# Seven block products instead of eight in three of the eleven units of each down-projection

## The chip, the cores and the metric

The kernel runs on one core of a Trainium2 chip. The metric is the device time of one execution in microseconds (us); lower is better. A core has a matrix engine (TensorE, "PE" in the profile; "PEld" is its load of the stationary operand), VectorE (DVE), ScalarE (ACT), GpSimd (POOL), and SyncE (SP), whose queue issues nearly all transfers from device memory here. TensorE writes its results to PSUM, which is split into eight banks of 128 x 512 f32 values.

## What is computed

Two layers of a decoder over 256 tokens with 1024 features. Each layer has an attention and a feed-forward part with a causal convolution of width 3; a final norm ends it. The change is in the last product of the feed-forward part, `@ w_down`, with 2816 rows of weights and 1024 columns:

```python
def conv_ffn(h, w_up, conv_w, conv_b, w_down):
    S_ = h.shape[1]
    u = h @ w_up
    up = jnp.pad(u, ((0, 0), (CONV_W - 1, 0), (0, 0)))
    u = conv_b + sum(conv_w[j] * up[:, j:j + S_] for j in range(CONV_W))
    gate, val = jnp.split(u, 2, axis=-1)
    return (jax.nn.silu(gate) * val) @ w_down
...
        x = x + conv_ffn(rmsnorm(x, ffn_norm[l]), w_up[l], conv_w[l], conv_b[l], w_down[l])
```

## The kernel before

**Numbers in two parts.** Every f32 operand of a product is split into a high part, rounded to the type that TensorE multiplies, and a low part, the rest. A product of two operands takes three matmuls: high by high, high by low, low by high.

**Weights.** All weights come as units of 128 x 2048 f32 (1 MB) from one packed array, in the order of use. `fetch(i)` (L165 to L170) issues the transfer of a unit into one of 3 raw buffers `wr`. `prepare(i)` (L197 to L217) makes the parts: ScalarE copies raw to high (`hi_part`, L181), VectorE takes raw minus high (`lo_part`, L189, or L191 where a gain is multiplied in, as in the units of the K/V projection), in 2 or 4 pieces; the last step fetches unit i+3. There are 4 buffers for the high and 4 for the low parts, `wh` and `wl`. `used(i)` says that TensorE has taken its last matmul of unit i and starts `prepare(i + 4)`. So a unit's parts can be written as soon as the unit four places before it is consumed.

**Order.** The program is written against a planned clock that counts ideal TensorE time (`tick`). Side work is put on a list as a `chain` of steps with due times; a step's instructions are emitted when the planned clock passes them, or at once where `need` or `require` asks for them. Each engine then runs its own instructions strictly in the order of emission, as early as their inputs and buffers allow. Steps of `prepare` start no closer than 4500 ns to each other by this clock (L203).

**The feed-forward part** (`ffn`, L661 to L761). 22 up units make gate and value features, 48 matmuls of 256 columns each. `post` (L700 to L732) follows each: three taps of the convolution (ACT L715, DVE L719 and L721), the Silu on ACT (L725), the product with the value on POOL (L726), and the split into parts, hi on ACT (L730) and lo on DVE (L731). Two consecutive results share a tile of 128 x 1024, a "quad", of which the pool has 15. Then `Down` (L569) runs the 11 down units. A down unit has 2 blocks of 128 rows (k), each with 1024 columns, that is two column halves n of 512; the activations have two blocks b of 128 tokens. That makes 2 x 2 x 2 = 8 block products, 24 matmuls with 512 columns (L587, L588, L590), added up over all units in four PSUM banks `acc[b][n]`. `units` runs units 0 to 8; `finish` runs units 9 and 10 bank by bank, and as each bank is complete `add` (L652) adds it to the residual `xr` on VectorE and starts what follows (`after`: squares for the norm on ACT, transposes on TensorE (L288) and their split into parts, on ACT L297 and DVE L298). In layer 0 the K/V projection follows (L345 to L347); in layer 1 the final norm, with POOL multiplying by the final gain (L1057). Four further PSUM banks, tags `u` and `t` with two each, serve the up units and the transposes; between unit 0 and the first `after` of a down-projection nobody uses them.

Of the kernel before, what the change touches and what calls it, by code (L numbers as in the profile page):

```python
# [51 lines left out]
U_DN0 = U_UP0 + NF  # L52
U_KV = U_DN0 + NF // 2
U_QB = U_KV + 2
U_OB = U_QB + 4
U_UP1 = U_OB + 4
U_DN1 = U_UP1 + NF
N_UNITS = U_DN1 + NF // 2


@with_exitstack
def trunk(ctx: ExitStack, tc, x, xw, pos, cpk, fin, w, out):
# [116 lines left out]
    def hi_part(i, c):  # L179
        g = gain_of(i, c)  # L180
        nc.scalar.activation(wq[i][0][:, c], raws[i][:, c], AF.Copy, **({} if g is None else {"scale": g}))  # L181
# [41 lines left out]
    def need(i):  # L223
        require("w", i)
# [344 lines left out]
    class Down:  # L569


        def __init__(self, u, n_u, parts, wait, short=False):
            self.u, self.n_u, self.parts, self.wait, self.short = u, n_u, parts, wait, short
            self.acc = None

        def mm(self, i, k, b, cols, last=1):
            if self.acc is None:
                self.acc = [[bank("acc") for _ in range(2)] for _ in range(NB)]
            need(self.u + i)
            self.wait(i)  # L580
            hi, lo = wq[self.u + i]
            ph, pl = self.parts[2 * i + k]
# [8 lines left out]
            tick(len(cols) * 3 * 512 / 2.4)  # L591

        def units(self, lo, hi):
            for i in range(lo, hi):
                for k in range(2):
                    for b in range(NB):
                        self.mm(i, k, b, range(2))
                        yield 6 * 512 / 2.4
                used(self.u + i)

        def finish(self, i0, after, tail=None, by_half=False):
# [26 lines left out]
            for i in range(i0, self.n_u):  # L628
                used(self.u + i)

        def end(self, b, n, tail):
# [4 lines left out]
            nc.vector.tensor_tensor(out=x_, in0=self.acc[b][n], in1=x_, op=ALU.add)  # L636
            need(self.u + i)
            self.wait(i)
            wh, wl = wq[self.u + i]
            for m in range(2):  # L640
# [20 lines left out]
    def ffn(layer, u_up, u_dn, hT, y, rb, after, tail=None):  # L661
# [37 lines left out]

        def post(i, up, pq):  # L700
            hi, lo = pq[:, 2 * (i % 2)], pq[:, 2 * (i % 2) + 1]
            t = [row3(S) for _ in range(2)]
            gs, h = row3(S), row3(S)
            w0, w1, w2, bb = ([cp[:, CW + (layer * 2 * NF + j * NF + i) * 4 + k:][:, :1] for j in range(2)] for k in range(4))
# [19 lines left out]
            def gate():  # L724
                nc.scalar.activation(gs, t[0], AF.Silu)  # L725
                nc.gpsimd.tensor_tensor(out=h, in0=gs, in1=t[1], op=ALU.mult)  # L726

            steps = [(200.0, scale), (700.0, tap2)] if i < n_raw else [(200.0, tap2)]
            chain(("p", i), *steps, (400.0, taps), (1600.0, gate),
                  (3400.0, lambda: nc.scalar.activation(hi, h, AF.Copy)),  # L730
                  (450.0, lambda: nc.vector.tensor_tensor(out=lo, in0=h, in1=f(hi), op=ALU.subtract)))  # L731
            parts.append((hi, lo))  # L732

        pq = quad()
# [9 lines left out]
        for i in range(2, NF):  # L744
            if i % 2 == 0:
                pq = quad()
# [5 lines left out]
        def wait(i):  # L752
            require("p", 2 * i)
            require("p", 2 * i + 1)

        if tail is not None:
            nc.sync.dma_start(fin_t, fin.partition_broadcast(P))
        dn = Down(u_dn, NF // 2, parts, wait, tail is not None)
        for _ in dn.units(0, NF // 2 - 2):
# [346 lines left out]
def pack(inp):  # L1106
# [19 lines left out]

    def rows2(mat):
        mm = k_major(mat)
        for i in range(mm.shape[0] // 2):
            units.append(turns(mm[2 * i:2 * i + 2]).transpose(1, 0, 2).reshape(P, UNIT))  # L1130

# [8 lines left out]
    up(inp["w_up"][0])  # L1140
    rows2(inp["w_down"][0])
    halves(turns(k_major(inp["w_kv_b"])))
# [6 lines left out]
    up(inp["w_up"][1])  # L1149
    rows2(inp["w_down"][1])  # L1150
    assert len(units) == N_UNITS
    wpk = np.stack(units)
# [39 lines left out]
```

## Time and profile before

| what | value |
|---|---|
| median of 3 runs (lowest, highest) | 547.92 us (547.56, 548.28) |
| span of the profiled execution | 545.6 us |
| granted TensorE clock, mean | 0.998 |
| down-projection of layer 0 in the profile | 230.6 to about 288 us |
| matmuls, and loads of the stationary operand | 3742 and 3742 |
| bytes read from device memory | 99.30 MB |

The profile is of one execution. Its span runs from the first to the last instruction; no time of its own is given for that execution beyond the span, so the 2.3 us between span and median are what lies around it. Busy time of TensorE counts overlapping, pipelined matmuls, so the distance between the starts of matmuls says more than their durations (379 ns for 512 columns). A group's "idle before" is time in which the engine stood still before instructions of the group, and the name behind it is who ended the wait.

### The profile page before, as it was taken

The page shows a single profiled execution, that of the slowest core. Times are in us where ns is not written, and L with a number is a line of the kernel's source. Part 1 is how long each engine was busy: PE and PEld are TensorE (multiplying, and loading weights), DVE is VectorE, ACT ScalarE, POOL GpSimd, SP SyncE. Part 2 cuts the span into 40 slices and gives each one's busy share as a digit, 9 for nine tenths or more (in the row PEclk, how much of TensorE's full clock was granted, in tenths as well). Part 3 has the DMA queues.
Part 4 walks back from the last instruction along what each step waited for, and adds up shares of the span by engine and source line. Part 5 has one row for each costly group of instructions (what it writes and reads, how often), then busy time and mean ns, then how long its engine had stood idle before and what let it go on. Part 6 is the DMA issues. An engine that isn't in the chain of part 4 may idle for free.

```text
span 545.6 us, 9917 instructions
## 1 busy us (share of the span) xinstructions
PE 537.5 (99%) x3742; PEld 493.9 (91%) x3742; DVE 416.9 (76%) x868; ACT 372.6 (68%) x731; POOL 131.6 (24%) x166
## 2 busy tenths in 40 slices
PE   8999999999999999999999999999999999999995
PEld 7888888899999999988888887789999999998884
DVE  6798778689798888864467788799899888884414
ACT  6989776678577777744357798797567777663314
POOL 8322102013322233220001165202332332210003
PEclk9999999999999999999999999999999999999999
DMA  8974445342556565666553534242375656666201
GB/s 317 401 268 175 167 154 181 129 155 79 199 211 217 223 220 195 208 227 231 178 208 135 179 150 156 77 155 91 142 264 201 214 193 217 249 229 220 109 0 77
DMA packets 16464, 100.99 MB, mean 185 GB/s; under 512 B 1952, under 2 KB 2080, under 8 KB 5920
## 3 DMA queue, kind: packets, MB, share of 16 engines
q1 hardware_dynamic: 16128, 100.09, 50.8%
q8 instruction: 29, 0.48, 0.3%
q10 hardware_dynamic: 288, 0.26, 0.1%
q14 instruction: 19, 0.16, 0.1%
HBM read 99.30 MB, written 1.05 MB: 184 GB/s over the span
## 4 chain that ended last, share of the span: by engine, by line
PE 90%; ACT 5%; DVE 3%; issue 1%; DMA 1%; DVEq 0%; POOL 0%; ACTq 0%
PE acc L590 8%; PE acc L587 8%; PE acc L588 8%; PE u L681 7%; PE u L682 7%; PE u L680 6%; PE t L681 6%; PE t L682 6%; PE t L680 6%; PE acc L345 5%; PE acc L346 5%; PE acc L347 5%; ACT m L468 2%; PE acc L792 2%; PE acc L682 2%; PE acc L681 2%
## 5 line engine op out<-in xcount | busy, mean ns | idle before, releaser
L189 DVE TENSOR_TENSOR wl<-wr,wh 128x1024 fp32r<-128x1024 f32 (+1 forms) x186 | 202.4, 1108 | 49.0 <-ACT wh L181 48.7
L181 ACT ACTIVATE wh<-wr 128x1024 fp32r<-128x1024 f32 (+1 forms) x190 | 176.5, 957 | 50.3 <-PE acc L590 42.2
L726 POOL TENSOR_TENSOR m<-m,m 128x256 f32<-128x256 f32 x44 | 69.1, 1571 | 167.8 <-DVE m L721 89.4
L587 PE MATMUL acc<-wh,q 128*128 128x512 f32 x238 | 92.2, 387 | 0.2 <-ACT q L545 0.2
L588 PE MATMUL acc<-wl,q 128*128 128x512 f32 x238 | 90.6, 381 | 0.0
L680 PE MATMUL u<-q,wh 128*128 128x256 f32 x320 | 88.3, 277 | 0.0
L681 PE MATMUL u<-q,wh 128*128 128x256 f32 x320 | 88.2, 276 | 0.1
L682 PE MATMUL u<-q,wl 128*128 128x256 f32 x320 | 87.9, 275 | 0.0
L680 PE MATMUL t<-q,wh 128*128 128x256 f32 x288 | 79.2, 275 | 0.0
L681 PE MATMUL t<-q,wh 128*128 128x256 f32 x288 | 79.2, 275 | 0.0
L682 PE MATMUL t<-q,wl 128*128 128x256 f32 x288 | 79.2, 275 | 0.0
L590 PE MATMUL acc<-wh,q 128*128 128x512 f32 x238 | 74.9, 380 | 0.0
L681 PEld LDWEIGHTS u<-q,wh 128*128 128x128 f32 x320 | 61.4, 192 | 0.3 <-DVE q L309 0.3
L682 PEld LDWEIGHTS u<-q,wl 128*128 128x128 f32 x320 | 61.4, 192 | 0.0
L680 PEld LDWEIGHTS u<-q,wh 128*128 128x128 f32 x320 | 61.3, 192 | 0.0
L680 PEld LDWEIGHTS t<-q,wh 128*128 128x128 f32 x288 | 55.3, 192 | 0.0
L681 PEld LDWEIGHTS t<-q,wh 128*128 128x128 f32 x288 | 55.3, 192 | 0.0
L682 PEld LDWEIGHTS t<-q,wl 128*128 128x128 f32 x288 | 55.3, 192 | 0.0
L587 PEld LDWEIGHTS acc<-wh,q 128*128 128x128 f32 x238 | 45.0, 189 | 7.0 <-ACT q L545 0.6
L590 PEld LDWEIGHTS acc<-wh,q 128*128 128x128 f32 x238 | 44.8, 190 | 6.2 <-issue 0.2
L588 PEld LDWEIGHTS acc<-wl,q 128*128 128x128 f32 x238 | 45.1, 189 | 5.8 <-issue 0.2
L345 PE MATMUL acc<-wh,q 128*128 128x512 f32 x128 | 50.0, 391 | 0.0
(182 smaller groups left out, 1008.7 us busy)
## 6 DMA issues: line engine op xcount, KB each, us to landing
wr<-in_w SPq DMA_DIRECT2D x82, 1024.0 KB, 4.8
wr<-in_w SPq DMA_DIRECT2D x16, 512.0 KB, 6.2
first<-in_xw SPq DMA_DIRECT2D x7, 384.0 KB, 6.0
xr<-in_x SPq DMA_DIRECT2D x2, 512.0 KB, 7.9
fin_t<-in_fin SPq DMA_DIRECT2D x1, 512.0 KB, 5.7
out<-ot SPq DMA_DIRECT2D x1, 512.0 KB, 2.6
first<-in_xw SPq DMA_DIRECT2D x1, 388.0 KB, 3.5
out<-m ACTq DMA_DIRECT2D x1, 256.0 KB, 2.1
```

The costliest lines, as they stand in the source:

```text
L181: nc.scalar.activation(wq[i][0][:, c], raws[i][:, c], AF.Copy, **({} if g is None else {"scale": g}))
L189: nc.vector.tensor_tensor(out=lo, in0=raw, in1=hi, op=ALU.subtract)
L345: nc.tensor.matmul(o, xh[:, blk(b)], wh, start=(c == 0), stop=False)
L346: nc.tensor.matmul(o, xh[:, blk(b)], wl, start=False, stop=False)
L347: nc.tensor.matmul(o, xl[:, blk(b)], wh, start=False, stop=(c == KC - 1))
L587: nc.tensor.matmul(o, ph[:, blk(b)], turns(hi[:, s_]), start=first, stop=False)
L588: nc.tensor.matmul(o, ph[:, blk(b)], turns(lo[:, s_]), start=False, stop=False)
L590: nc.tensor.matmul(o, pl[:, blk(b)], turns(hi[:, s_]), start=False, stop=end)
L680: nc.tensor.matmul(o, hi[:, s_], xh, start=(c == 0), stop=False)
L681: nc.tensor.matmul(o, hi[:, s_], xl, start=False, stop=False)
L682: nc.tensor.matmul(o, lo[:, s_], xh, start=False, stop=(c == KC - 1))
L726: nc.gpsimd.tensor_tensor(out=h, in0=gs, in1=t[1], op=ALU.mult)
```

## The change

In units 2, 5 and 8 of both down-projections, the 2 x 2 block product (token blocks by k blocks, times k blocks by column halves) is taken with seven block products after Strassen and Winograd instead of eight. With x0..x3 the activation blocks (k0 b0, k0 b1, k1 b0, k1 b1) and r0..r3 the weight blocks (k0 n0, k1 n0, k1 n1, k0 n1; the host packs those three units in this order), it forms

```
x4 = x0 - x1   x5 = x1 - x3   x6 = x0 - x5   x7 = x2 - x6
t0 = r0 + r3   t1 = r2 + r3   t2 = t0 + r2   t3 = t2 + r1
one = x0 r0   six = x6 t2   five = x5 t0   sev = x4 t1
acc00 += x2 r1   acc01 += x7 r2   acc10 += x3 t3
```

The sums of weights t0..t3 become a unit of their own, right behind the unit they are made from (`slot`, `SUMS`). It is not transferred: its raw buffer is filled by VectorE from the neighbouring raw buffer, three instructions of 1024, 512 and 512 columns (`sum_of`). Of the unit with r0..r3 only 1536 of its 2048 columns are split into parts, since r3 enters no product by itself; all of the sum unit is. POOL makes x4..x7 (`mix`) in the up stage; the split of all eight blocks, 1024 columns, is one ACT and one DVE instruction at the start of the down stage or later (`split`), in place of the four of L730 and L731. The four extra products add up over the three units in the four banks of tags `u` and `t`; after unit 8 `gather` adds them to `xr`: one copy on ACT, five instructions on DVE, three on POOL, all of 512 columns. The planned distance of 4500 ns between preparations is 2500 ns for the unit behind a sum unit.

```diff
+SEVEN = ((2, 5, 8), (2, 5, 8))
...
+SUMS = [slot(l_, i_) + 1 for l_ in range(2) for i_ in SEVEN[l_]]
...
-                nc.sync.dma_start(raws[i][:, c], w[i][:, c])
+                if i not in SUMS:
+                    nc.sync.dma_start(raws[i][:, c], w[RAW[i]][:, c])
+
+    def sum_of(i, to, a, k):
+
+        src, t = (raws[j].rearrange("p (k n) -> p k n", k=4) for j in (i - 1, i))
+        n = to.stop - to.start
+        nc.vector.tensor_tensor(out=t[:, to], in0=(t if n == 1 else src)[:, a],
+                                in1=src[:, k:k + 1].to_broadcast([P, n, 512]), op=ALU.add)
...
-        w_time[0] = max(clock[0] + 200.0, w_time[0] + 4500.0, 34000.0 if i == 7 else 0.0)
+        w_time[0] = max(clock[0] + 200.0, w_time[0] + (2500.0 if i - 1 in SUMS else 4500.0), 34000.0 if i == 7 else 0.0)
...
+        if i + 1 in SUMS:
+            cut[1] = slice(UNIT // 2, 3 * UNIT // 4)
+            steps = [(w_time[0] - clock[0], first), (300.0, lambda: sum_of(i + 1, slice(0, 2), slice(0, 3, 2), 3)),
+                     (900.0, lambda: lo_part(i, cut[0])), (300.0, lambda: hi_part(i, cut[1])),
+                     (600.0, lambda: sum_of(i + 1, slice(2, 3), slice(0, 1), 2)),
+                     (600.0, lambda: sum_of(i + 1, slice(3, 4), slice(2, 3), 1))]
         chain(("w", i), *steps, (2000.0 / n, last))
...
+        def seventh(self, i):
+
+            u = self.at(i)
+            need(u)
+            need(u + 1)
+            self.wait(i)
+            if not self.more:
+                self.more = [bank(t) for t in ("u", "t", "u", "t")]
...
+            for o, x_, hi, lo, k, mine in ((one, 0, rh, rl, 0, True), (six, 6, th, tl, 2, True), (five, 5, th, tl, 0, True),
+                                           (sev, 4, th, tl, 1, True), (a00, 2, rh, rl, 1, False), (a01, 7, rh, rl, 2, False),
+                                           (a10, 3, th, tl, 3, False)):
+                o, wh, wl = pairs(o), turns(hi[:, half(k)]), turns(lo[:, half(k)])
+                c = blk(x_)
+                nc.tensor.matmul(o, xh[:, c], wh, start=mine and own["start"], stop=False)
+                nc.tensor.matmul(o, xh[:, c], wl, start=False, stop=False)
+                nc.tensor.matmul(o, xl[:, c], wh, start=False, stop=mine and own["stop"])
+                tick(3 * 512 / 2.4)
+            if own["stop"]:
+                self.gather()
+
+        def gather(self):
...
+            chain(("more",), (100.0, lambda: nc.scalar.activation(v_, one, AF.Copy)),
+                  (100.0, add(dve, x00, one, x00)), (500.0, add(dve, v_, six, v_, ALU.subtract)),
+                  (500.0, add(dve, w_, five, v_)), (400.0, add(pool, x01, x01, w_)),
+                  (100.0, add(dve, z_, sev, v_, ALU.subtract)), (100.0, add(dve, x11, x11, sev, ALU.subtract)),
+                  (400.0, add(pool, x10, x10, z_)), (400.0, add(pool, x11, x11, w_)))
+
         def units(self, lo, hi):
             for i in range(lo, hi):
+                if self.layer is not None and i in SEVEN[self.layer]:
+                    self.seventh(i)
+                    used(self.at(i))
+                    used(self.at(i) + 1)
+                    yield 21 * 512 / 2.4
+                    continue
...
+        def mix(pq):
+
+            x = pq.rearrange("p c (b t) -> p (c b) t", b=NB)
+            for o, a, b in ((4, 0, 1), (5, 1, 3), (6, 0, 5), (7, 2, 6)):
+                nc.gpsimd.tensor_tensor(out=x[:, o], in0=x[:, a], in1=x[:, b], op=ALU.subtract)
+
+        def split(i):
+
+            raw, hi, lo = parts[2 * i], quad(), quad()
+
+            def high():
+                wait(i, False)
+                nc.scalar.activation(hi, raw, AF.Copy)
+
+            parts[2 * i] = tuple(t.rearrange("p c t -> p (c t)") for t in (hi, lo))
+            chain(("a", i), (5000.0 * (i - 2) + 300.0, high),
+                  (800.0, lambda: nc.vector.tensor_tensor(out=lo, in0=raw, in1=f(hi), op=ALU.subtract)))
```

More of the change, by code (lines that the diff above doesn't have):

```diff
@@ L57, with slot @@
 U_DN1 = U_UP1 + NF
-N_UNITS = U_DN1 + NF // 2
+N_UNITS = U_DN1 + NF // 2 + len(SEVEN[1])
+def slot(layer, i):
+    return (U_DN0, U_DN1)[layer] + i + sum(k < i for k in SEVEN[layer])
+SUMS = [slot(l_, i_) + 1 for l_ in range(2) for i_ in SEVEN[l_]]
+RAW = {}
+for k_ in range(N_UNITS):
+    if k_ not in SUMS:
+        RAW[k_] = len(RAW)
 @with_exitstack
@@ L569, in trunk, with __init__ @@
     class Down:
-        def __init__(self, u, n_u, parts, wait, short=False):
-            self.u, self.n_u, self.parts, self.wait, self.short = u, n_u, parts, wait, short
-            self.acc = None
+        def __init__(self, u, n_u, parts, wait, short=False, layer=None):
+            self.u, self.n_u, self.parts, self.wait, self.short, self.layer = u, n_u, parts, wait, short, layer
+            self.acc, self.more = None, None
         def mm(self, i, k, b, cols, last=1):
@@ L591, in mm, with at @@
             tick(len(cols) * 3 * 512 / 2.4)
+        def at(self, i):
+            return self.u + i if self.layer is None else slot(self.layer, i)
+        def seventh(self, i):
[5 more added lines that the diff above has]
+                self.more = [bank(t) for t in ("u", "t", "u", "t")]
+            one, five, six, sev = self.more
+            (rh, rl), (th, tl) = wq[u], wq[u + 1]
+            xh, xl = self.parts[2 * i]
+            (a00, a01), (a10, _) = self.acc
+            own = dict(start=i == SEVEN[self.layer][0], stop=i == SEVEN[self.layer][-1])
+            for o, x_, hi, lo, k, mine in ((one, 0, rh, rl, 0, True), (six, 6, th, tl, 2, True), (five, 5, th, tl, 0, True),
[9 more added lines that the diff above has]
+                self.gather()
@@ new lines, in gather, with add @@
+        def gather(self):
+            one, five, six, sev = self.more
+            v_, w_, z_ = (mid() for _ in range(3))
+            (x00, x01), (x10, x11) = ([xr[b][:, half(n)] for n in range(2)] for b in range(NB))
+            def add(eng, out, a, b, op=ALU.add):
+                return lambda: eng.tensor_tensor(out=out, in0=a, in1=b, op=op)
+            dve, pool = nc.vector, nc.gpsimd
+            chain(("more",), (100.0, lambda: nc.scalar.activation(v_, one, AF.Copy)),
[3 more added lines that the diff above has]
+                  (400.0, add(pool, x10, x10, z_)), (400.0, add(pool, x11, x11, w_)))
@@ L700, in post @@
         def post(i, up, pq):
+            seven = i // 2 in SEVEN[layer]
             hi, lo = pq[:, 2 * (i % 2)], pq[:, 2 * (i % 2) + 1]
             t = [row3(S) for _ in range(2)]
-            gs, h = row3(S), row3(S)
+            gs = row3(S)
+            h = pq[:, i % 2] if seven else row3(S)
             w0, w1, w2, bb = ([cp[:, CW + (layer * 2 * NF + j * NF + i) * 4 + k:][:, :1] for j in range(2)] for k in range(4))
@@ L728, in post @@
             steps = [(200.0, scale), (700.0, tap2)] if i < n_raw else [(200.0, tap2)]
+            if seven:
+                chain(("p", i), *steps, (400.0, taps), (1600.0, gate), *([(1500.0, lambda: mix(pq))] if i % 2 else []))
+                parts.append(pq)
+                return
             chain(("p", i), *steps, (400.0, taps), (1600.0, gate),
@@ L745, in ffn @@
             if i % 2 == 0:
-                pq = quad()
+                pq = quad(F32 if i // 2 in SEVEN[layer] else F32R)
             up = bank("acc" if i < 4 else "t" if i % 2 else "u")
@@ L750, in ffn, with wait @@
             post(i, [up[:, :S], up[:, S:]], pq)
-        def wait(i):
+        def wait(i, whole=True):
             require("p", 2 * i)
             require("p", 2 * i + 1)
+            if whole and i in SEVEN[layer]:
+                require("a", i)
         if tail is not None:
             nc.sync.dma_start(fin_t, fin.partition_broadcast(P))
-        dn = Down(u_dn, NF // 2, parts, wait, tail is not None)
+        dn = Down(u_dn, NF // 2, parts, wait, tail is not None, layer)
+        for i in SEVEN[layer]:
+            split(i)
         for _ in dn.units(0, NF // 2 - 2):
@@ L1125, in halves, with rows2 @@
             units.append(blk[4 * a:4 * a + 4].transpose(1, 0, 2).reshape(P, UNIT))
-    def rows2(mat):
+    def rows2(mat, seven=()):
         mm = k_major(mat)
         for i in range(mm.shape[0] // 2):
-            units.append(turns(mm[2 * i:2 * i + 2]).transpose(1, 0, 2).reshape(P, UNIT))
+            m = turns(mm[2 * i:2 * i + 2]).transpose(1, 0, 2).reshape(P, 4, 512)
+            units.append((m[:, [0, 2, 3, 1]] if i in seven else m).reshape(P, UNIT))
     def up(mat):
@@ L1149, in pack @@
     up(inp["w_up"][1])
-    rows2(inp["w_down"][1])
-    assert len(units) == N_UNITS
+    rows2(inp["w_down"][1], SEVEN[1])
+    assert len(units) == len(RAW)
     wpk = np.stack(units)
```

16 lines of the change are left out of this document (8 added, 8 removed).

## The prediction

> **What bounds the kernel now.** I read first the page's busy times, its chain and the waits of TensorE, for the whole execution.
>
> ```profile
> span 545.6 us, 9917 instructions
> PE 537.5 (99%) x3742; PEld 493.9 (91%) x3742; DVE 416.9 (76%) x868; ACT 372.6 (68%) x731; POOL 131.6 (24%) x166
> ...
> PE 90%; ACT 5%; DVE 3%; issue 1%; DMA 1%; DVEq 0%; POOL 0%; ACTq 0%
> ...
> PE u L275 <- DVE warm L251: 1.1, 1, 1.1
> PE acc L792 <- ACT q L836: 0.3, 1, 0.3
> PE u L493 <- ACT m L478: 0.2, 1, 0.2
> PE acc L587 <- ACT q L545: 0.2, 1, 0.2
> ```
>
> TensorE is never short of work: it waited 1.8 us in all, most of it at the start, and none of that in a down-projection. Busy matmuls overlap, though, so the question is what one of them costs. The order of time of TensorE's instructions answers it; here are the first of a down-projection and the first ones of the second and the eighth group of six.
>
> ```profile
> 230.55 0.38 PE L587 MATMUL acc<-wh,q 128*128 128x512 f32 x1
> ...
> 231.84 0.38 PE L587 MATMUL acc<-wh,q 128*128 128x512 f32 x1
> ...
> 239.62 0.38 PE L587 MATMUL acc<-wh,q 128*128 128x512 f32 x1
> ```
>
> From 230.55 to 239.62 lie 7 groups of six, 42 matmuls: 9.07 / 42 = 0.216 us from start to start, though each shows 0.38. A unit of 24 takes 5.18 us. Next, the table by stage: the last up unit's start to the third down unit, the middle of the down-projection, its last two units (columns: stage, its length, then busy time and instructions of PE, PEld, DVE, ACT, POOL).
>
> ```profile
> 225.20:240.90 15.70, 15.70 (x98) 14.43 (x97) 12.62 (x19) 9.70 (x15) 5.45 (x11) 1.00 0.60 206
> 240.90:272.00 31.10, 31.10 (x146) 27.22 (x145) 14.16 (x12) 12.01 (x12) 0.00 (x0) 1.00 0.59 205
> 277.20:287.60 10.40, 10.40 (x53) 8.90 (x52) 6.75 (x16) 5.63 (x13) 0.55 (x1) 1.00 0.51 197
> ```
>
> In the middle VectorE is busy for 14.16 of 31.10 us, ScalarE for 12.01, POOL not at all. The reader is to see two things: taking matmuls away shortens the path one for one, and the work put in their place falls where those engines have room. Only the first and last stages are crowded.
>
> **What the change removes.** Three matmuls in each of 6 units: 18 x 0.216 = **3.89 us**. The 21 that remain have the same form, 512 columns with a load of the stationary operand each, as the 24 had.
>
> **What it adds on VectorE and ScalarE.** These rows give the prices (group, count, busy us, mean ns):
>
> ```profile
> L189 DVE TENSOR_TENSOR wl<-wr,wh 128x1024 fp32r<-128x1024 f32 x12 | 14.2, 1222 | 16.6 <-ACT wh L181 16.6
> L181 ACT ACTIVATE wh<-wr 128x1024 fp32r<-128x1024 f32 x12 | 12.0, 1048 | 18.6 <-PE acc L590 18.6
> ...
> L189 DVE TENSOR_TENSOR wl<-wr,wh 128x512 fp32r<-128x512 f32 x44 | 28.7, 686 | 5.8 <-ACT wh L181 5.6
> L181 ACT ACTIVATE wh<-wr 128x512 fp32r<-128x512 f32 x44 | 25.6, 639 | 4.2 <-PE acc L347 1.9 <-PE acc L590 1.7 <-DMA wr<-in_w 0.2
> L308 DVE CAST q<-y 128x256 fp32r<-128x256 f32 x16 | 4.3, 286 | 0.0
> ```
>
> An add with a repeated operand is not in the trace. The nearest row with two f32 inputs in SBUF is L189, so I take 1.22 + 0.69 + 0.69 = 2.60 us for the three sums of a unit. Below it could be the one-input cast, 286 ns for 256 columns, or 2.3 us for 2048; above I allow twice L189, 5.2 us. A period of two ordinary units and one seven-product unit then lasts 2 x 5.18 + 21 x 0.216 = 14.90 us. In it VectorE has 4.88 (two ordinary units) + 1.91 (lo of 1536 columns) + 2.60 (sums) + 2.44 (lo of the sum unit) + 1.22 (lo of the activations) = 13.05 us: 88%, tight but enough. ScalarE has 4.19 + 1.69 + 2.10 + 1.05 = 9.03 us.
>
> **Whether the sum unit is in time.** The raw unit R and its sum unit T hold two of four part buffers and are freed together, at the end of their 21 matmuls. The next pair must be ready two ordinary units later, 10.36 us, and T itself 0.65 us after that, since the first of the seven products reads only R. How long a preparation starts after its buffer is freed, the order of time of ScalarE shows:
>
> ```profile
> 241.11 2.00 ACT L181 ACTIVATE wh<-wr 128x1024 fp32r<-128x1024 f32 x2 [2.72 <-PE acc L590]
> 246.29 2.00 ACT L181 ACTIVATE wh<-wr 128x1024 fp32r<-128x1024 f32 x2 [3.18 <-PE acc L590]
> ```
>
> It waits for TensorE and starts at once (5.18 us apart). The first sum needs only raw data and can be done before the buffer is free. The rest stands in VectorE's order: hi 1.05, then lo of R 1.22, the activations' lo 1.22, two sums 1.38, lo of R 0.69, two lo of T 2.44: 8.0 us of 11.0. With sums at twice the price it is 9.4, or 11.8 if the first is not early. Behind a late T stand, on VectorE, the lo of the next ordinary units; they have 5 us more.
>
> The raw data of the next R is issued when T's last lo frees a raw buffer, 8.0 us after the release, and takes
>
> ```profile
> DMA to landing us min/median/max: 4.7/4.8/6.4
> ```
>
> so it lands at 12.8 to 14.4 us of a period of 14.9. It is in time, by 0.5 to 2.1 us. SP issues no more transfers than before, as the sum unit has none.
>
> The first pair of a layer is made while the last up units are worked off: 12.62 of 15.70 us, plus 2.60 for sums, 1.22 for the activations, less 0.53 (1.22 - 0.69 of R): 15.9 us. But 2.44 us of that belong to the unit after it, needed 4.5 us later, so T is ready some 13.5 us into 15.7. What hides these sums is the 3.1 us that VectorE had left there; gone, they would cost their own excess, unit by unit.
>
> **The activations.** In the up stage a seven-product unit drops two pairs of L730 and L731 and gets four POOL subtractions of 128 columns.
>
> ```profile
> L731 DVE TENSOR_TENSOR q<-m,q 128x256 fp32r<-128x256 f32 x44 | 18.4, 421 | 19.9 <-ACT q L730 19.9
> L730 ACT ACTIVATE q<-m 128x256 fp32r<-128x256 f32 x44 | 18.1, 415 | 43.6 <-POOL m L726 43.5
> L463 POOL TENSOR_TENSOR m<-m 128x128 f32<-128x128 f32 x16 | 8.0, 505 | 12.9 <-ACT m L468 12.8
> L726 POOL TENSOR_TENSOR m<-m,m 128x256 f32<-128x256 f32 x44 | 69.1, 1571 | 167.8 <-DVE m L721 89.4
> ```
>
> Four times 0.505 (L463), at most half of L726's 1.571 each, make 2.0 to 3.1 us on an engine that was idle 167.8 us before L726. VectorE and ScalarE get 0.84 and 0.83 us less. The next product with the value queues behind them on POOL; its result is needed a whole stage later. I cost it at nothing.
>
> **Gather and handover, the crowded place.** Prices of its nine instructions of 512 columns:
>
> ```profile
> L636 DVE TENSOR_TENSOR xr<-acc,xr 128x512 f32<-128x512 f32 x1 | 0.7, 692 | 0.5 <-PE acc L590 0.5
> L923 ACT ACTIVATE m<-acc,rstd 128x512 f32<-128x512 f32 x8 | 5.4, 682 | 0.3 <-PE acc L347 0.2
> L187 POOL TENSOR_TENSOR wl<-wr,wh 128x512 fp32r<-128x512 f32 x8 | 10.1, 1283 | 12.9 <-ACT wh L181 12.9
> ```
>
> Five on DVE are 3.45 us, one on ACT 0.68, three on POOL 3.85. In layer 1 they lie beside an idle VectorE:
>
> ```profile
> 533.06 0.76 DVE L656 TENSOR_TENSOR xr<-acc,xr 128x256 f32<-128x256 f32 x2 [10.80 <-PE acc L590]
> ```
>
> It had stood still for 10.80 us, and the last bank is added 8 to 9 us after the gather begins; POOL's part ends after about 5. Cost: nothing. In layer 0 the last two units' 10.40 us held 6.75 us of VectorE's work. The gather adds 3.45, and the first K/V unit moves in as well: unit 8 now frees both its buffers at its end, so a preparation that ran at 272.95, a unit earlier, falls into this stage.
>
> ```profile
> 272.95 2.74 DVE L191 SCALAR_TENSOR_TENSOR wl<-wr,cp,wh 128x512 fp32r<-128x512 f32 x4 [2.49 <-ACT wh L181]
> ...
> 281.25 0.76 DVE L656 TENSOR_TENSOR xr<-acc,xr 128x256 f32<-128x256 f32 x2 [0.39 <-PE acc L590]
> ...
> 283.00 0.60 PE L288 MATMUL t<-ident,xr 128*128 128x128 f32 x4
> ```
>
> That makes 6.75 + 3.45 + 2.74 = 12.94 us in 10.40: 2.54 us too much. What gives way: the gather's first steps, on banks that are complete before the unit's end, can run up to 1 us early; the second K/V unit is needed only 12 matmuls (2.6 us) into the projection; and the transposes at 283.00 stand 1.0 us behind the add that they need (281.25 + 0.76). Behind a late add stand those transposes, and in TensorE's queue all matmuls after them. I take 0.4 us of stall, between 0 and 2.54, near zero because the leeways together exceed the excess.
>
> **The sum.** 545.6 - 3.89 + 0.4 = 542.1 us of span; the median of the runs lies 2.3 us over the span, which does not change: **544.4 us**.
>
> **Rivals.** (1) The handover overflows: all 2.54 us show, 547.92 - 3.89 + 2.54 = 546.6. For it speaks the order of VectorE's work, by due time and not by urgency; against it the leeways. (2) POOL's adds hold VectorE up there as well. The trace has such a case (POOL and DVE in order of time):
>
> ```profile
> 226.22 0.73 POOL L726 TENSOR_TENSOR m<-m,m 128x256 f32<-128x256 f32 x1 [3.39 <-DVE m L721]
> 226.37 1.67 DVE L189 TENSOR_TENSOR wl<-wr,wh 128x1024 fp32r<-128x1024 f32 x1 [0.31 <-ACT wh L181]
> ```
>
> The subtraction took 1.67 us instead of 1.22 when it began 0.15 us behind POOL's product. If one of POOL's three adds holds VectorE for its full 1.28 us on top of the overflow, the gain is gone: 547.9. Against it, VectorE's own five instructions of the gather each read one operand from PSUM, as L636 does; only the parts of the K/V units beside them have both in SBUF, as this L189 has. The Trainium skill, "SBUF — State Buffer", section "SBUF: two separate sides", states that VectorE instructions with two SBUF inputs and POOL instructions take a shared port pair as an exclusive lock, for a whole instruction. By that rule all three adds could block, and the time would be above 547.9; the pair of rows above agrees with a lock, as VectorE lost 0.45 us of the 0.58 that POOL still had to go.
>
> (3) The other side: the sum unit is late each time. If its steps, on ACT and DVE in turn, did not overlap at all, the chain would be 8.0 + 1.22 (first sum) + 0.64 + 2 x 1.05 + 1.05 (the other hi parts) = 13.0 us against 11.0, and TensorE would stand still for 2.0 us at the second and third pair of each layer, four times: 547.92 - 3.89 + 8.0 = 552.0. It decides from 1.0 us of lateness on (3.89 / 4), a chain of 12.0 us. For it speaks VectorE at 88%; against it that the chain's two engines ran ahead of one another in every unit before. (4) The 21 matmuls run slower, for they change the PSUM bank with each product. If 42 changes cost 0.08 us each, 3.4 us, the time is 547.4. Against it: L587 and L588 change banks every second matmul at 0.216 us.
>
> **How the numbers follow.** Forecast 0.75 (543.5 to 545.6), rival 1 0.09, rival 2 0.05, rival 3 0.06, rival 4 0.05. A measurement of this kernel can tell about 0.2%, 1.1 us, from no change: faster is below 546.8, slower above 549.0. Faster: 0.75 + most of rival 1, 0.07 = 0.82; slower: rival 3, 0.06; the same: the rest, 0.12. The range runs from 543.5 (no stall, the runs' own spread of 0.4) to 546.6 (rival 1's price); rivals 2 to 4 are left out, 0.16.
>
> **What would show it.** Per step: 18 matmuls fewer; 0.216 us from start to start in the seven-product units; no wait of TensorE for `wh` or `wl` there; VectorE near 88% in the middle of a down-projection; sums of 1.22 and 0.69 us; in layer 0's last two units VectorE over 90% and a gap of a few tenths of a us before transposes. Wrong it would be if TensorE waits at the first matmul on a sum unit, if sums take near twice their price, or if the K/V projection starts with gaps of more than 1 us.

## The result, and the profile after

The changed kernel takes **552.73 us** (median of 4 runs, 552.51 to 554.76) against 547.75 us for the kernel before: 1.0101 times as long, interval 1.0083 to 1.0118. The forecast was 544.4 us, 543.5 to 546.6. The profiled execution took 552.88 us with a span of 551.2 us. The first lines of its page:

```profile
span 551.2 us, 9986 instructions
PE 537.0 (97%) x3724; PEld 492.4 (89%) x3724; DVE 453.7 (82%) x902; ACT 382.1 (69%) x739; POOL 161.6 (29%) x196
...
PEclk9999999999999999999989999999999999999997
...
PE 45%; DVE 24%; ACT 10%; POOL 8%; issue 7%; DMA 4%; POOLq 0%; DVEq 0%; ACTq 0%; SPq 0%
```

18 matmuls are gone (3742 to 3724), but the chain that ended last lies on TensorE for 45% of the span, where it was 90%: VectorE, ScalarE, POOL and transfers now make up as much of it. The granted clock falls below 9 twice: in slice 21 (275.6 to 289.4 us), and in the last one, where the work ends. The waits of TensorE (what waited for what: us in total, times, longest):

```profile
PE t L315 <- DVE xr L733: 3.6, 1, 3.6
PE u L302 <- DVE warm L278: 1.1, 1, 1.1
PE acc L615 <- DVE wl L210: 0.5, 1, 0.5
```

The second line was there before. The first is new: transposes for the K/V projection waited 3.6 us for a half bank of the residual (L656 before, L733 now). The third is the only new wait at a weight part that the view lists; it is at the last unit of layer 1.

**Where the time came from.** Each TensorE instruction of the trace before has its counterpart after; the distance between the two starts, followed through the execution, changes at these places (after minus before, worked out from the starts):

```
+0.36  first 9 us        } before any seven-product unit
+0.34  at 54 us          }
-1.94  the three seven-product units of layer 0
+5.54  layer 0's handover to the K/V projection (275.7 to 290)
-1.94  the three of layer 1
+0.41  second pair of layer 1 (513)
+0.80  last unit of layer 1 (536)
+2.0   from the last matmul to the end
=5.6   551.2 - 545.6
```

So the whole expected gain, 3.89 us, is there. Three things took it back: 5.54 us in one place of layer 0, 1.2 us in layer 1, 2.0 us in the tail. The 0.70 us at the top has no seven-product unit near it. It is part of how executions differ: the first down unit began at 230.55 us before and at 231.25 after, but at 230.49 in a later run of the changed kernel that leaves out only the gather; and 19 executions of the kernel before on one chip range from 547.28 to 548.19 us. The profiled one of before was among the short ones (545.6 us of span; all runs whose time and span are both listed have 1.7 to 1.8 us around the span), so the medians differ by 5.0 and not 5.6 us.

**The place in layer 0.** First the table by stage of the changed kernel: two periods with seven-product units, then the handover (stage, length, busy time and instructions of PE, PEld, DVE, ACT, POOL, then clock, DMA share, GB/s).

```profile
241.60:271.40 29.80, 29.80 (x139) 26.08 (x138) 27.02 (x28) 17.36 (x19) 8.02 (x9) 1.00 0.52 190
280.00:285.00 5.00, 1.92 (x9) 1.33 (x8) 5.00 (x5) 2.40 (x4) 3.94 (x3) 1.00 0.47 195
285.00:290.00 5.00, 4.46 (x16) 3.67 (x17) 4.25 (x12) 2.76 (x8) 0.00 (x0) 0.66 0.45 161
```

In the two periods TensorE never stands: 29.80 / 138 = 0.216 us from start to start. VectorE is at 27.02 / 29.80 = 91%. Then TensorE is busy for 1.92 of 5 us, and in the 5 us after that its clock is 0.66. The chain of waits in this window says why (start, us, what):

```profile
268.84 4.74 DMA wr<-in_w
...
273.96 1.07 ACT wh L202
...
275.06 1.23 DVE wl L210
...
281.64 3.51 DVE wl L212 x3
285.15 0.35 DVE xr L733
...
285.54 1.08 PE t L315 x4
286.62 0.43 PE acc L614
```

It begins with a **transfer**: the raw data of the last down unit, issued at 268.84. VectorE in order of time shows what that does (the bracket is the idle time before, and what ended it):

```profile
275.06 1.23 DVE L210 TENSOR_TENSOR wl<-wr,wh 128x1024 fp32r<-128x1024 f32 x1 [2.87 <-ACT wh L202]
276.20 0.68 DVE L655 TENSOR_TENSOR xr<-u,xr 128x512 f32<-128x512 f32 x1
...
279.73 1.39 DVE L212 SCALAR_TENSOR_TENSOR wl<-wr,cp,wh 128x512 fp32r<-128x512 f32 x1
281.05 0.67 DVE L655 TENSOR_TENSOR xr<-xr,t 128x512 f32<-128x512 f32 x1
281.64 3.51 DVE L212 SCALAR_TENSOR_TENSOR wl<-wr,cp,wh 128x512 fp32r<-128x512 f32 x3
285.07 0.74 DVE L733 TENSOR_TENSOR xr<-acc,xr 128x256 f32<-128x256 f32 x2
```

VectorE, at 91% just before, stood idle for 2.87 us. Then the low part of the late unit, the gather (L655) and four low parts of K/V units (L212) ran in one row, and the add of the first half bank (L733) came last, at 285.07. Its input was long there: the matmuls of that bank were done at about 279.8. ScalarE and POOL in that stretch:

```profile
273.96 1.06 ACT L202 ACTIVATE wh<-wr 128x1024 fp32r<-128x1024 f32 x1 [3.93 <-DMA wr<-in_w]
```

```profile
279.30 4.64 POOL L655 TENSOR_TENSOR xr<-xr,m 128x512 f32<-128x512 f32 x3 [29.68 <-DVE m L655]
```

ScalarE waited 3.93 us for the transfer, with its target free since 271.4, the end of unit 7. POOL's three adds took 4.64 us, 1.55 each, and lay from 279.30 to 283.94, beside those parts L212.

**Why the transfer was late.** There are three raw buffers. A sum unit occupies one, filled by VectorE, while its source occupies another until its own last low part has read it, and that stands on VectorE behind the three sums: the raw data of unit 8 landed at 262.34 and was released at 268.78, 6.4 us later. The transfer at 268.84 is the one that waited for this buffer. In the kernel before, ScalarE made the high part of the same unit as soon as TensorE freed its target:

```profile
267.01 2.00 ACT L181 ACTIVATE wh<-wr 128x1024 fp32r<-128x1024 f32 x2 [3.18 <-PE acc L590]
```

The name in the bracket is TensorE's; the raw data was there, since 265.01.

### The profile page after: what moved, and what is told of

Same layout as the page of the kernel before. It is cut to its first block, busy times and chain, and to the rows that moved or that the text cites. A ratio compares the mean times of both kernels' runs of the same rounds, so it can differ in the third digit from the quotient of the medians.

```text
span 551.2 us, 9986 instructions
## 1 busy us (share of the span) xinstructions
PE 537.0 (97%) x3724; PEld 492.4 (89%) x3724; DVE 453.7 (82%) x902; ACT 382.1 (69%) x739; POOL 161.6 (29%) x196
## 4 chain that ended last, share of the span: by engine, by line
PE 45%; DVE 24%; ACT 10%; POOL 8%; issue 7%; DMA 4%; POOLq 0%; DVEq 0%; ACTq 0%; SPq 0%
DVE wl L210 9%; POOL m L805 6%; PE acc L372 5%; PE acc L374 5%; PE acc L373 5%; ACT wh L202 5%; DMA wr<-in_w 4%; DVE m L800 4%; DVE m L798 3%; PE u L758 3%; PE u L759 2%; PE u L757 2%; ACT m L495 2%; PE acc L897 2%; PE acc L617 2%
## 5 line engine op out<-in xcount | busy, mean ns | idle before, releaser
L210 DVE TENSOR_TENSOR wl<-wr,wh 128x1024 fp32r<-128x1024 f32 (+1 forms) x198 | 211.6, 1089 | 29.1 <-ACT wh L202 28.7
L202 ACT ACTIVATE wh<-wr 128x1024 fp32r<-128x1024 f32 (+1 forms) x202 | 185.9, 949 | 34.9 <-DMA wr<-in_w 19.9
L805 POOL TENSOR_TENSOR m<-m,m 128x256 f32<-128x256 f32 x32 | 51.5, 1610 | 129.7 <-DVE m L800 75.3
L614 PE MATMUL acc<-wh,q 128*128 128x512 f32 x190 | 74.5, 392 | 0.2 <-ACT q L572 0.2
L615 PE MATMUL acc<-wl,q 128*128 128x512 f32 x190 | 73.1, 385 | 0.5 <-DVE wl L210 0.5
L617 PE MATMUL acc<-wh,q 128*128 128x512 f32 x190 | 60.9, 382 | 0.0
L372 PE MATMUL acc<-wh,q 128*128 128x512 f32 x128 | 50.0, 391 | 0.0
L813 ACT ACTIVATE q<-m 128x256 fp32r<-128x256 f32 x32 | 13.1, 415 | 53.1 <-POOL m L805 53.1
L373 PE MATMUL acc<-wl,q 128*128 128x512 f32 x128 | 48.8, 381 | 0.0
L374 PE MATMUL acc<-wh,q 128*128 128x512 f32 x128 | 48.6, 380 | 0.0
```

The source lines that it names most:

```text
L210: nc.vector.tensor_tensor(out=lo, in0=raw, in1=hi, op=ALU.subtract)
L372: nc.tensor.matmul(o, xh[:, blk(b)], wh, start=(c == 0), stop=False)
L373: nc.tensor.matmul(o, xh[:, blk(b)], wl, start=False, stop=False)
L374: nc.tensor.matmul(o, xl[:, blk(b)], wh, start=False, stop=(c == KC - 1))
L614: nc.tensor.matmul(o, ph[:, blk(b)], turns(hi[:, s_]), start=first, stop=False)
L615: nc.tensor.matmul(o, ph[:, blk(b)], turns(lo[:, s_]), start=False, stop=False)
```

## Theories

The first theory, from the prediction's own doubts, was that the last two units of layer 0 are **overfull**: gather, K/V parts and POOL's adds, more work than time. The rival was that what comes there comes **late**: the sum unit holds a raw buffer, transfers run late behind it, and VectorE first waits and then works in a burst. (Where the first expectations say only A and B, A is the first and B the second.) A further question is the order of VectorE's work: half adds behind low parts that are needed later.

Beside each run stands its median, and its ratio to runs of the kernel before on the same chip (medians 547.57 to 547.71) with the interval.

## Experiments: which layer, which part

**Layer 0 alone.**

```diff
-SEVEN = ((2, 5, 8), (2, 5, 8))
+SEVEN = ((2, 5, 8), ())
```

> Seven products in layer 0 alone, layer 1 as before. Theory A (the time went at the handover from the down-projection to the K/V projection: VectorE's work of the gather, POOL's adds and the K/V preparation in one place): layer 0 gives 1.94 us and loses 5.5 us, so about 551.3 us. Theory B (the raw buffers: the sum unit takes one of three, so transfers are late in both layers, and the places where TensorE stands still are only where it shows): the same place stalls, 551.3 us too, but with the wait of ScalarE for the last unit's transfer (3.9 us) as its start. If the 0.7 us that the changed kernel was late before its first seven-product unit is part of the change it stays here.

Measured: 551.52 us, 1.0064 [1.0047, 1.0081].

**Layer 1 alone.**

```diff
+SEVEN = ((), (2, 5, 8))
```

> Seven products in layer 1 alone. Both theories: 1.94 us gained, 0.4 us lost where TensorE waits at the second pair, 0.8 us at the last unit's lo part, 2.0 us in the tail behind the last matmul: about 549.0 us. If instead layer 1's losses came only from running later, it is 546 us.

Measured: 548.56 us, 1.0015 [1.0006, 1.0024]. The differences of the medians, 3.88 and 0.92 us, add up to 4.80 of the 4.98 of both. The layers lose separately; net of what the missing matmuls give, layer 0 loses four times as much.

**Two units in each layer, without unit 8.**

```diff
+SEVEN = ((2, 5), (2, 5))
```

> Units 2 and 5 alone have seven products in both layers; unit 8 is as before, so the gather begins three units (15 us) ahead of the handover, and the last unit's transfer is no longer behind a sum unit. 12 matmuls fewer are 2.59 us. Theory A: the handover is as before, 547.75 - 2.59 + 0.4 (second pair of layer 1) = 545.6 us. Theory B (lateness of transfers carries through): the stalls move to units 8 to 10, 547 us or more.

Measured: 545.44 us, 0.9955 [0.9940, 0.9970], as the first theory has it: 12 matmuls fewer are worth 2.59 us, and 2.20 arrive. The view lists one wait of 0.2 us at the handover. Seven-product units as such cost nothing; the one that ends two units before the handover does. But this takes gather and late transfer away from there together, so it doesn't tell them apart.

**No gather** (the four extra banks are left out of the residual).

```diff
-            if own["stop"]:
-                self.gather()
```

> The changed kernel without the gather: the sums of the four extra banks are left out of the output, all else stays. Theory A (gather and POOL's adds are what is too much): the handover stall of 5.5 us and the tail's 2.0 us go, about 545 us. Theory B (late transfer of the last unit): ScalarE still waits for it and the K/V units still crowd; of the 5.5 us some 2 to 3 stay, 547.5 us.

Measured: 545.78 us, 0.9965 [0.9952, 0.9978]; between the two, nearer to the first theory. The waits of TensorE at the handover:

```profile
PE t L315 <- DVE xr L731: 1.2, 1, 1.2
...
PE t L315 <- DVE q L325: 0.3, 1, 0.3
```

With nothing of the gather left, the transposes are still late. The tail is 6.4 us from the last matmul to the end, as before the change, so its 2.0 us come by the gather.

**No POOL adds** (the last three of the gather's steps are left out of the residual).

```diff
-                  (500.0, add(dve, w_, five, v_)), (400.0, add(pool, x01, x01, w_)),
+                  (500.0, add(dve, w_, five, v_)),
...
-                  (400.0, add(pool, x10, x10, z_)), (400.0, add(pool, x11, x11, w_)))
```

> The changed kernel without the three adds on POOL; what they add is left out of the output. If POOL's adds are what is late or hold VectorE up (K/V parts took 1.17 to 1.75 us beside them instead of 0.75, 2 us in all, and the adds to xr wait for them), some 4 of the gather's 7 us go: about 548.5 us. If it is VectorE's five instructions and their place behind the last unit's parts, 551 us.

Measured: 549.66 us, 1.0039 [1.0024, 1.0054], 3.1 us under the changed kernel. The gap in layer 0 goes from 3.62 to 2.13 us, and the tail from 8.3 to 7.3. POOL's adds cost time, but they aren't the greater part.

**POOL's adds on VectorE instead.**

```diff
-            dve, pool = nc.vector, nc.gpsimd
+            dve, pool = nc.vector, nc.vector
```

> The three adds of the gather on VectorE instead of POOL, nothing left out: VectorE has 2.1 us more to do, and nobody holds it up; the tail no longer has POOL's final gain behind them. If contention and POOL's slowness are what costs, 549.5 us; if VectorE's load in the last two units is the bound, 553 us or more.

Measured: 552.01 us, 1.0079 [1.0062, 1.0095]. It fits neither: three instructions more on VectorE cost about what the three beside it on POOL cost. The gap in layer 0 goes to 2.02 us, but the tail from 8.3 to 9.1. Moving the adds is no cure.

**Seven-product units one place earlier,** so that gather and last sum unit lie 5 us further from the handover.

```diff
+SEVEN = ((1, 4, 7), (1, 4, 7))
```

> Units 1, 4 and 7 have seven products instead of 2, 5 and 8, so the gather begins one ordinary unit (5.2 us) ahead of the last two, and the first K/V unit is prepared there too. All 18 matmuls are saved. Theory A (crowding of VectorE in the last two units): about 15.4 us of VectorE's work now has 15.6 us, the handover costs some tenths, and the tail is as before: 547.6 - 3.9 + 0.6 = 544.3 us. Theory B (lateness of transfers): the last unit is still fetched behind a sum unit; stalls of 2 us or more stay, 546 us or more.

Measured: 548.00 us, 1.0012 [0.9999, 1.0025]. The first theory's number, 544.3, is missed, the late theory's holds. The gather began a unit earlier, and transposes still waited:

```profile
PE t L315 <- DVE xr L733: 1.5, 1, 1.5
...
PE u L643 <- DVE q L833: 0.9, 2, 0.5
```

The high parts of the last two units waited 3.43 and 1.33 us for transfers here too. The second line is new, and in neither theory: the split of the activations is late at the first seven-product unit, which is now unit 1. The ten runs range from 547.07 to 549.78 us, more than those of the kernel before.

## Experiments: the raw buffers

**Sums in the source's own raw buffer.** The sum unit takes no buffer, and VectorE makes four sums of 512 columns in place. In this run they may be made before the source's parts are taken, so the values multiplied are not all the reference's; the amount of work is kept.

```diff
+        if i in SUMS:
+            raws[i] = raws[i - 1]
...
+        for k, a in ((0, 3), (3, 2), (2, 0), (1, 2)):
+            nc.vector.tensor_tensor(out=r[:, k], in0=r[:, k], in1=r[:, a], op=ALU.add)
```

> The sums are made in the raw buffer of the unit they come from, after its parts are taken, so a sum unit holds no raw buffer of its own and transfers run one unit further ahead; VectorE makes four sums of 512 columns, 2.7 us instead of 2.6. Theory B: the last unit is in time, the gather starts 3 us earlier, the handover stall falls from 5.5 to about 2 us and the waits for lo parts in layer 1 (1.2 us) go: about 548 us. Theory A: the crowd in the last two units stays, 551.5 us or more.

Measured: 547.78 us, 1.0007 [0.9995, 1.0020]: 4.95 us less than the changed kernel, with a sum more in each unit and the whole gather. That is the late theory's number, as a median of ten runs from 546.36 to 549.62 us.

**Sum unit transferred.** Its raw buffer receives the source unit's values once more and no sums are made, so the products are not those of the sums.

```diff
-                if i not in SUMS:
-                    nc.sync.dma_start(raws[i][:, c], w[RAW[i]][:, c])
+                nc.sync.dma_start(raws[i][:, c], w[RAW[i - (i in SUMS)]][:, c])
```

> The sum unit is transferred like the others, and VectorE's sums are left out: its values are those of the unit before it, so the products are not the sums'. Three raw buffers, 6 MB more to transfer, 2.6 us less on VectorE in each of six units. If VectorE's sums are the root: 547 us. If the raw buffer is: 551 us or more, with ScalarE's wait for the last unit's transfer as before.

Measured: 546.02 us, 0.9965 [0.9952, 0.9978]. Six transfers more make it faster, and this is the number expected if VectorE's sums are the root. The loaded unit takes a raw buffer as the sum unit did, and yet the last unit's data landed at 268.51, 5 us earlier: without the sums in front of its last low part, unit 8 gave its buffer back 4.0 us after landing (259.49 to 263.50) instead of 6.4. So a third buffer that is held is not by itself what costs; the sums that lengthen the hold belong to it.

**Four raw buffers.** The space comes from the pool of quads, 13 instead of 15.

```diff
-    qd = ctx.enter_context(tc.tile_pool(name="qd", bufs=15))
+    qd = ctx.enter_context(tc.tile_pool(name="qd", bufs=13))
...
-            raws[i] = wp.tile([P, UNIT], F32, tag="raw", name=f"wr{i}", bufs=3)
+            raws[i] = wp.tile([P, UNIT], F32, tag="raw", name=f"wr{i}", bufs=4)
```

> The changed kernel with four raw buffers instead of three; to make room the pool of quads has 13 instead of 15. If the sum unit's hold on a raw buffer is the root of the late transfers, the last unit is in time, layer 1 loses nothing (3.2 us) and the handover loses 2 us less: about 547.7 us. If VectorE's sums are (they delay the release of every raw buffer), it stays at 551 us or more.

Measured: 546.25 us, 0.9974 [0.9964, 0.9984], 6.5 us under the changed kernel and below the expected 547.7. Not one instruction of the sums or the gather was touched, so the sums by themselves are not the root either: a buffer more, or no sums, each removes the lateness. ScalarE's waits for raw data, in the changed kernel and then with four buffers:

```profile
ACT wh L202 <- DMA wr<-in_w: 19.9, 8, 4.0
```

```profile
ACT wh L202 <- DMA wr<-in_w: 0.6, 1, 0.6
```

The last unit lands at 269.81, before its part buffers are free, and ScalarE now waits for TensorE, as in the kernel before:

```profile
271.20 1.06 ACT L202 ACTIVATE wh<-wr 128x1024 fp32r<-128x1024 f32 x1 [3.13 <-PE acc L617]
```

**Control:** the same exchange of buffers in the kernel before.

> The kernel before with four raw buffers and 13 quads, no seven-product unit: what this exchange of buffers does by itself. Both theories: 547.6 us, within 0.5; above that, the two quads that are missing cost it.

Measured: 548.02 us, 1.0007 [0.9997, 1.0016]. A fourth buffer by itself is worth nothing; it is worth 6.5 us where a sum unit made by VectorE holds one. With it TensorE still waits 1.3 and 0.4 us at the handover, for an add (L733) and for a part of the transposed values (L325); the same two waits stand in the run with the transferred sum unit.

## Experiments: the order of VectorE's work

**VectorE by due time** from the gather to the end of layer 0's feed-forward part, that is, in the order in which the program lists the steps.

```diff
+                if self.layer == 0:
+                    ordered.enter_context(tc.manual_schedule(engines={mybir.EngineType.DVE}))
...
+        ordered.close()
```

> The changed kernel with VectorE's instructions in the order in which the kernel's own list emits them, from the gather to the end of layer 0's down-projection. In the changed kernel three parts of the first K/V unit and one of the second stand ahead of the first add to xr, though they fall due after it: the scheduler moved them. If that order is what TensorE waited for, the 3.6 us before the first transposes go to some tenths and the whole is about 549.5 us. If VectorE is only overloaded there, the wait moves to the next transposes and to the K/V projection: 552 us or more.

Measured: 549.15 us, 1.0034 [1.0021, 1.0048], as expected of it, 3.6 us under the changed kernel. The description of the kernel before said that each engine runs its instructions in the order of emission. For VectorE this is wrong outside stretches that are ordered by hand: with the list's order pinned, the first half add runs ahead of the second, third and fourth K/V part:

```profile
280.58 0.74 DVE L737 TENSOR_TENSOR xr<-acc,xr 128x256 f32<-128x256 f32 x2
281.24 1.74 DVE L212 SCALAR_TENSOR_TENSOR wl<-wr,cp,wh 128x512 fp32r<-128x512 f32 x1
```

Without it the scheduler of the kernel's framework had put them in front. The late transfer is still there, though, and a wait comes back one step further on:

```profile
PE t L315 <- DVE q L325: 1.8, 1, 1.8
```

**In place and by due time,** with the sums after the source's parts.

```diff
+        need(i - 1)
         r = raws[i].rearrange("p (k n) -> p k n", k=4)
```

> Sums in place (e8; here a sum unit also waits for the parts of its source, which e8 didn't keep) together with the order by due time (e9). If late transfers and order are the two causes, all of layer 1's losses and nearly all of layer 0's go: 547.6 - 3.9 + 0.8 + some tenths, 544.7 us. If the last two units are overloaded in any order, 546.5 us or more.

Measured: 546.26 us, 0.9976 [0.9965, 0.9987], between the numbers expected. Sums that wait for their source's parts make the sum unit itself late: by the distances of the starts TensorE lost 2.4 us at low parts of sum units, and it waited 0.8 at the transposes. The profiled execution, 547.71 us, is the longest of ten (545.23 to 547.71), so the median run will have lost less.

**The same with units 1, 4 and 7.**

> Units 1, 4 and 7 with sums in place and the order by due time. The handover's 2.4 us of e5 go; the waits of 0.6 us for the activations' lo part at the first of the three units stay in each layer: 545.2 us. If the late transfers still set the handover: 547 us.

Measured: 550.49 us, 1.0051 [1.0034, 1.0069], a miss. In each layer the first seven-product unit stood 2.2 us for a PSUM bank of tag `t`, which the taps of the last up units were still reading:

```profile
PE t L642 <- DVE m L803: 4.4, 2, 2.2
```

The place of the units is bounded on both sides: by the up stage's banks in front and by the handover behind.

**Units 2 and 5 in layer 0, all three in layer 1, sums in place.**

> Units 2 and 5 of layer 0, units 2, 5 and 8 of layer 1, sums in place. 15 matmuls fewer are 3.24 us. With no K/V units behind layer 1 and the last unit in time, nothing is left to stall: 547.6 - 3.24 + 0.4 = 544.8 us. If the gather itself is too much for the last two units even without K/V units beside it, layer 1 loses 2 us: 546.5 us.

Measured: 545.87 us, 0.9968 [0.9958, 0.9979]; again between, with 1.1 us lost at low parts of sum units, which the expectation had at 0.4.

**Four raw buffers and VectorE by due time:** the two cures together, each of which had left a remainder.

> Four raw buffers and 13 quads (e13) with VectorE's order by due time from the gather on (e9). If these are the two causes: 547.6 - 3.9 + 1 = 544.7 us. If the quads cost (see the next run), so much more.

Measured: **544.26 us, 0.9934 [0.9920, 0.9949]**, faster than both kernels, and at the time that had been forecast for the change. All the waits of TensorE that the view lists:

```profile
PE u L302 <- DVE warm L278: 1.1, 1, 1.1
PE u L520 <- ACT m L505: 0.2, 1, 0.2
PE acc L616 <- ACT q L572: 0.2, 1, 0.2
```

None is left at the handover. VectorE there, in order of time:

```profile
272.74 1.23 DVE L210 TENSOR_TENSOR wl<-wr,wh 128x1024 fp32r<-128x1024 f32 x1 [2.67 <-ACT wh L202]
...
277.41 1.40 DVE L212 SCALAR_TENSOR_TENSOR wl<-wr,cp,wh 128x512 fp32r<-128x512 f32 x1
...
280.06 0.76 DVE L737 TENSOR_TENSOR xr<-acc,xr 128x256 f32<-128x256 f32 x2 [0.66 <-PE acc L619]
280.74 1.01 DVE L212 SCALAR_TENSOR_TENSOR wl<-wr,cp,wh 128x512 fp32r<-128x512 f32 x1
```

The last unit's part is made 2.3 us earlier (272.74 for 275.06), and the add now waits for TensorE, not TensorE for the add. The stage is nearly full here too: VectorE is busy for 9.3 of the 10 us from 275 to 285. The sum comes out: 547.66 (the kernel before on that chip) less 3.89, plus 0.2 at the handover and 0.4 in the tail (6.7 us, as in the control with 13 quads), is 544.4.

## Why the prediction was wrong, point by point

**The matmuls removed: right.** 18 fewer, 0.216 us each in the periods above; the two layers show -1.94 us each, as 9 x 0.216.

**The prices: nearly right.** The changed kernel's groups (count, busy us, mean ns), the activations' differences, then the sums:

```profile
L821 POOL TENSOR_TENSOR q<-q 128x128 f32<-128x128 f32 x24 | 18.8, 784 | 1.9
...
L190 DVE TENSOR_TENSOR wr<-wr,wr 128x512 f32<-128x512 f32 x12 | 9.1, 756 | 0.2
...
L190 DVE TENSOR_TENSOR wr<-wr 128x1024 f32<-128x1024 f32 x6 | 7.3, 1222 | 0.3 <-DMA wr<-in_w 0.2
```

The sums of a unit take 1.22 + 2 x 0.756 = 2.73 us, forecast 2.60. Four differences take 3.14 us, the top of the forecast 2.0 to 3.1; no wait of TensorE comes of them where the units are 2, 5 and 8. VectorE was forecast at 88% and is at 91%.

**"Whether the sum unit is in time": the step that failed.** It followed the part buffers, and one raw transfer, that of the next R, to land "in time, by 0.5 to 2.1 us". TensorE indeed hardly waits at sum units (0.4 us in all, at the second pair of layer 1). But of three raw buffers two are tied up around each pair, longer than usual as the sums stand in front of the low parts that release them, and the units behind a pair are issued late; the step never followed the ordinary ones. The one that counts is the last of layer 0, whose data landed 2.2 us after its parts could have been written (273.6 against 271.4). An average of 91% hid that VectorE first stood for 2.87 us. That it stood is not the loss: with both cures it stands for 2.67 us at the same place, but works again 2.3 us sooner, and ScalarE in front of it waits for TensorE and not for a transfer. Four raw buffers, which change just this, give back 6.5 us.

**"Gather and handover": 0.4 us forecast, 5.54 measured.** Its balance, 12.94 us of work in 10.40, assumed work that could begin at the start of the stage, and leeways of which the first was that the gather runs up to 1 us early. It ran late, behind the low part of the late unit. The second leeway, that the second K/V unit is needed later, was lost to the order: parts ran ahead of the half adds. With both mended the leeways do cover the excess, and the handover loses 0.2 us. The prediction's own sign of being wrong, gaps of more than 1 us there, is what came. And a price was missing altogether, that of what a stall does to the clock: of the 5.54 us, 3.62 are the wait, and most of the rest is matmuls and transposes at half pace after it, 0.43 us instead of 0.216 for a matmul.

**Layer 1 at nothing: 3.2 us measured.** The prediction looked at VectorE, idle for 10.80 us, and at the last bank. The same lateness moved the gather there:

```profile
536.53 3.75 POOL L655 TENSOR_TENSOR xr<-xr,m 128x512 f32<-128x512 f32 x3 [36.16 <-DVE m L655]
540.25 2.52 POOL L1162 TENSOR_TENSOR xf<-xr,fin_t 128x512 f32<-128x512 f32 x2
```

POOL's adds end at about 540.25, and only then can it multiply by the final gain. ScalarE's scaling and squares wait behind, and from the last matmul to the end it takes 8.3 us where it took 6.4. That it is the lateness and not the gather as such shows with four raw buffers: with the whole gather it takes 6.7 us.

**The rivals.** The overflow (546.6) came closest as to place, but its 2.54 us were the excess of work, not a delay and a slow clock. POOL's adds (547.9) are real at both ends, 3.1 us in all. The late sum unit gave 552.0, near the time measured, by another mechanism: it had TensorE standing four times at sum units, and of those waits only the 0.4 us in layer 1 are there. Bank changes cost nothing that shows: 0.216 us from start to start in the periods above.

**What surrounds the span.** The 2.3 us between span and median were two things: 1.7 us around every span, and a profiled execution 0.6 us shorter than the median.

Open: what makes executions differ by up to 0.7 us before the changed units, why the tail is longer with POOL's adds on VectorE, and why runs of some of the kernels spread over 2.5 us and more.

## What to carry to other kernels

When a derived tile takes a place in a rotating set of transfer buffers, follow every transfer behind it, not only the next of its own kind: count from which instruction to which a buffer is held, with the new work that stands in front of its release, and see when the last unit of the stage lands. A share of busy time says nothing about whether the work could begin in time; look at what ends the idle time in front of the crowded stage, a transfer or the engine that is meant to set the pace. And where two cures each leave a remainder (a buffer, an order), try them together before judging the change.

## What the hardware showed

**A short stall costs twice.** After 3.62 us without a matmul, TensorE's matmuls of 512 columns came at twice their distance:

```profile
286.84 0.63 PE L615 MATMUL acc<-wl,q 128*128 128x512 f32 x1
287.26 0.63 PE L617 MATMUL acc<-wh,q 128*128 128x512 f32 x1
287.69 0.63 PE L614 MATMUL acc<-wh,q 128*128 128x512 f32 x1
```

0.43 us apart, until 289.4. Without POOL's adds, after a wait of 2.13 us at the transposes, the granted clock also fell:

```profile
284.00:286.00 2.00, 1.87 (x7) 1.52 (x8) 2.00 (x7) 1.51 (x5) 0.00 (x0) 0.56 0.00 0
286.00:288.00 2.00, 2.00 (x9) 1.68 (x8) 1.25 (x4) 1.07 (x4) 0.00 (x0) 0.59 1.02 262
```

With POOL's adds on VectorE, 2.02 us sufficed (0.60 and 0.54 in the same two stretches). With VectorE by due time, after 1.83 us, it did not fall:

```profile
284.00:286.00 2.00, 1.21 (x8) 1.09 (x9) 1.98 (x6) 1.13 (x4) 0.00 (x0) 1.00 0.00 0
286.00:288.00 2.00, 2.00 (x11) 1.76 (x10) 2.00 (x6) 0.29 (x1) 0.00 (x0) 1.00 0.47 66
```

The Trainium skill, "TensorE: Matmul & The Clock Gate", section "What's actually happening", has TensorE at half rate after an idle window of about 3.4 us. The doubled distance agrees; that about 2 us sufficed twice does not fit a plain threshold of 3.4 us of stall. By the distances of the starts the handover lost 4.2 us with the wait of 2.13, and 2.3 us with the one of 1.83.

**POOL's adds beside VectorE.** The five K/V parts around the gather, and all such parts in the kernel before:

```profile
L212 DVE SCALAR_TENSOR_TENSOR wl<-wr,cp,wh 128x512 fp32r<-128x512 f32 x5 | 5.6, 1157 | 0.0
```

```profile
L191 DVE SCALAR_TENSOR_TENSOR wl<-wr,cp,wh 128x512 fp32r<-128x512 f32 x24 | 16.9, 753 | 7.9 <-ACT wh L181 7.9
```

1157 ns on average instead of 753, while POOL's adds took 1.55 us, against 1.28 in the prediction's row for L187. Both engines lengthen. In layer 1, where VectorE's instructions beside them each read one operand from PSUM, the same three adds took 3.75 us, 1.25 each. The Trainium skill, "SBUF — State Buffer", section "SBUF: two separate sides", gives the rule that the prediction weighed, a lock for a whole instruction; longer instructions on both sides agree with taking turns, and leaving the adds out gave 3.1 us over both layers.
